# Units made by ScalarE, the second group's P5 and P4 by quarters, and a new written order, in a two-level Strassen matmul

## The chip, the cores and the metric

The kernel runs on one core of one Trainium2 chip. The metric is device time in microseconds of one execution, the median of three runs. A core has TensorE (PE in the profile: matmuls into PSUM; PEld: its weight loads), VectorE (DVE), ScalarE (ACT), GpSimd (POOL), and SyncE (SP), whose queue issues all DMAs of this kernel. A granted clock of 1.00 means TensorE at full speed.

## The reference

```python
x: (8, 2048, 2048) float32    w: (2048, 2048) float32
cs = cumsum(x, axis=1)
diff = cs - concatenate([zeros, cs[:, :-1, :]], axis=1)
out = matmul(diff, w)                       # float32
```

The difference of neighbouring running sums is x itself, so the output is x @ w: 16384 rows by 2048 by 2048.

## The kernel before

**Tiling.** The 16384 rows are 128 row tiles of 128 rows. The first four (the `plain` rows, L302) are multiplied in bf16 without further tricks while w arrives: the prologue, period 0. It makes an identity matrix on DVE (`zeros`, `ones`, `numbers`, `numbers turned`, four times `eye`, L220 to L236), loads x in pieces (`first x.q.r`, L245) and w in halves of 128x1024 (`w.h.ko`, L281), casts x (`cast x`, DVE, L251), turns it on PE against the identity (`turn x`, L260; `turned`, L270), casts w on ScalarE (L287), and takes the largest absolute value of w (`max w`, DVE, L291). From that maximum come `uw` and its reciprocal `uinv`. PE runs 30 `warm` matmuls of zeros (L338) in the gaps before. When uinv is there, w is scaled and written as fp16 in place: the blocks B11, B21, B12, B22 (`block`, L415 on DVE, L417 on ScalarE). `left over` (L430) is a last piece of the plain rows, made from blocks B11 and B21.

The other row tiles go in groups of four, g, g+1, h = g+2 and h+1. A group's rows times w is done by one level of the Strassen-Winograd scheme, seven products for two pairs of row tiles: A11 B11 (called P1), A12 B21 (P2), S1 T1 (P5), S4 B22 (P3), A22 T4 (P4), S2 T2 and S3 T3. S1 to S4 are sums of blocks of x, T1 to T4 of w. A product takes row tiles g and h with the same right operand. It is done in one of two ways. A `Whole` product is 32 matmuls of 128x512 (`matmuls`, L529). A `Quarters` product applies the same scheme once more, 28 matmuls (`quarter`, L551): seven slots of four matmuls, in exchange for DVE sums s1 to s4 of left operands, two DVE additions in PSUM (`middle`, `last`), three copies on ScalarE (`first`, `out2`, `out4`, L568), and differences of the right operand. Right operands that stay are made once (`make_1` to `make_5` of the class `Seven`); others are made anew for each group, into one buffer `flow`, by `give` (Q1, Q3, Q4). All these DVE operations are recorded through one helper at L517.

The first group (period 0) does all its products whole. In the second (period 1) P1, P5 and P4 are whole, P2 and P3 by quarters. From the third on, all five named are by quarters; S2 T2 and S3 T3 are whole throughout. Periods 1 to 30 are one group each, period 31 the tail.

**Around the products.** Each row tile is loaded in two halves (`load`, L130), weighed (`weigh`, ScalarE, L138: mean of absolute values, collected by an accumulator), given a `mean` (DVE, L157), a `scale` (DVE, L159) and a `unit` (L160): `unit` is the mean times `uw`, a 128x1 tile, and with it results are scaled back. ScalarE narrows the scaled tile to fp16 (`narrow`, L170), and a transposing DMA turns it (`turn`, L187). Results are taken from PSUM by ScalarE (`keep`, L565) and DVE (`add`, L576, multiply and add), and stored (`put`, L584 and L596). A name such as unit5 counts the row tile from the first of the group in work: 4 to 7 belong to the next group. `keep C11h.0` is the first half of C11 of row tile h, `C11h+P2.h.1` the addition of P2's second half to it, `P5.s3` a sum and `P5.4` a slot of P5.

**Order.** Every operation is recorded with a label, and `emit` sorts them by period times PERIOD plus a place from tables written out by hand: one each for the periods 0, 1, 2, 29, 30, 31, and one, `None`, for all the others. So each engine's instructions, and SP's DMAs, stand in the order of these tables. Semaphore waits follow from the operands.

```python
record(f"unit{role(t)}", "pool", lambda: nc.gpsimd.tensor_scalar(u, m, uw, None, MUL))
...
def all_seven(g):
    return g > PLAIN + 4
```

Of the kernel before, what the change touches and what calls it, by code (L numbers as in the profile page):

```python
# [10 lines left out]
def kernel(  # L11
# [6 lines left out]
    nc = tc.nc  # L18
# [26 lines left out]
    PERIOD = 1600  # L45
# [74 lines left out]
    def role(t):  # L120
        return t - PLAIN - 4 * period[0]
# [26 lines left out]
    def scale_of(t):  # L148
        if t < END:
            m2 = sums_of.pop(t)  # L150
            m = means_at[t % 4]
            s = scales[t] = scales_at[t % 8]
            u = unit[t] = units_at[t % 8]
            record(
                f"mean{role(t)}",
                "dve",
                lambda: nc.vector.tensor_scalar(m, m2[:, :1], m2[:, 1:], TINY, ADD, MAX),  # L157
            )
            record(f"scale{role(t)}", "dve", lambda: nc.vector.reciprocal(s, m))  # L159
            record(f"unit{role(t)}", "pool", lambda: nc.gpsimd.tensor_scalar(u, m, uw, None, MUL))  # L160
# [443 lines left out]
    class Seven:  # L604
# [13 lines left out]
        def room(self):  # L618
            return [spare.pop(0) for _ in range(4)]
# [244 lines left out]
    def all_seven(g):  # L864
        return g > PLAIN + 4
# [15 lines left out]
    def group(g):  # L881
# [62 lines left out]
        if more:  # L944
            P5 = Quarters("P5", P2.banks, S1g, S1h, in_5, room(at))
        else:
            P5 = Whole("P5", P2.banks, S1g, S1h, T1)
# [12 lines left out]
        if more:  # L960
            in_5.give("Q3")
# [58 lines left out]
        if more:  # L1020
            P4 = Quarters("P4", P3.banks, A22g, A22h, in_4, room(at))
            P4.one()
            P4.two()
        else:
            P4 = Whole("P4", P3.banks, A22g, A22h, T4)
        in_3.give("Q3")
        if not more:
            make_5(in_5)
# [19 lines left out]
        if more:  # L1048
            in_4.give("Q1")
# [19 lines left out]
        if more:  # L1069
            in_4.give("Q3")  # L1070
# [25 lines left out]
        if next_g < END:  # L1096
            if all_seven(g + 4) and more:
                in_1.give("Q1")
# [15 lines left out]
        if not more:  # L1114
            make_3(in_4)
            in_1.give("Q1")
# [11 lines left out]
    for g in range(PLAIN + 4, END, 4):  # L1128
# [8 lines left out]
            'first x.0.2': 0, 'first x.1.1': 1, 'first x.0.0': 2, 'first x.1.3': 3,  # L1137
            'first x.0.3': 4, 'first x.0.1': 5, 'first x.1.2': 6, 'first x.1.0': 7, 'w.0.0': 8,
            'zeros': 9, 'ones': 10, 'numbers': 11, 'numbers turned': 12, 'eye': 13, 'eye#2': 14,
# [390 lines left out]
```

## Time and profile before

| | |
|---|---|
| runs | 1452.06 us median (1451.21, 1452.06, 1452.2) |
| profiled execution, its own time | 1451.33 us |
| its span | 1449.5 us |
| PE | 1440.0 us busy, 6706 matmuls |
| DVE | 1339.7 us busy, 2457 instructions |
| ScalarE | 1129.8 us busy, 1742 instructions |
| GpSimd | 43.3 us busy, 129 instructions |
| granted clock | 1.000 |
| DMA | 351.60 MB, 243 GB/s mean |

The span is what the profiler saw, from the first to the last instruction or transfer; the execution's own time has some 1.8 us more around it. Busy times are a mean over stages with different limits, so what holds PE up is read from its waits and from windows of single stages. A line of the lines' view reads: code line, engine, operation, output and input tiles, shape, count, then busy time and mean ns of one, then the idle time before, and what ended it. In a timeline, the first two numbers are the start and the length, and a bracket at the end gives the idle time ahead and what released it.

### The profile page before, as it was taken

The numbers are of one execution on the slowest core, as the hardware profiler recorded it, in microseconds if no ns is written. First come the engines' busy times: TensorE is split into PE (matmuls) and PEld (weight loads), VectorE is DVE, ScalarE is ACT, GpSimd is POOL, SyncE is SP. The second block draws the span as 40 slices with busy tenths as digits, with TensorE's granted clock in tenths as the row PEclk, the third lists the DMA queues.
The fourth block names the chain that finished last, engine by engine and source line by source line (L and its number), as shares of the span: only waits on it lengthen the run. The fifth ranks groups of instructions, "written<-read, shape, count | busy, mean of one in ns | idle before, by whom it ended". The sixth has DMA issues, their size and how long they took to land.

```text
span 1449.5 us, 20480 instructions
## 1 busy us (share of the span) xinstructions
PE 1440.0 (99%) x6706; PEld 653.6 (45%) x6706; DVE 1339.7 (92%) x2457; ACT 1129.8 (78%) x1742; POOL 43.3 (3%) x129
## 2 busy tenths in 40 slices
PE   8999999999999999999999999999999999999998
PEld 4444444444444444444444444444444444444443
DVE  6998899999999999999999999999999999999998
ACT  5987678887778877778877788877788777788773
POOL 0000000000000000000000000000000000000000
PEclk9999999999999999999999999999999999999999
DMA  9999978999888899988898888998889988888973
GB/s 362 375 263 263 245 200 235 237 252 252 232 222 240 238 263 238 235 220 236 242 273 224 227 233 239 252 249 229 227 238 237 265 243 230 216 242 241 273 204 111
DMA packets 343788, 351.60 MB, mean 243 GB/s; under 512 B 270976, under 2 KB 270976, under 8 KB 343680
## 3 DMA queue, kind: packets, MB, share of 16 engines
q1 hardware_dynamic: 343680, 350.29, 88.5%
q8 instruction: 52, 0.85, 0.2%
q14 instruction: 56, 0.46, 0.1%
HBM read 150.99 MB, written 134.22 MB: 197 GB/s over the span
## 4 chain that ended last, share of the span: by engine, by line
PE 98%; DMA 2%; DVE 0%; ACT 0%; SPq 0%; issue 0%; DVEq 0%; ACTq 0%
PE b L551 61%; PE b L529 33%; PE b L302 3%; DMA W<-in_w_dram 1%; DMA W<-in_x_dram 0%; PE b L430 0%; DVE arena L576 0%; SPq L245 0%; ACT arena L287 0%; PE b L260 0%; DVE b L517 0%; ACT arena L565 0%; DVEq L1525 0%; ACTq L287 0%
## 5 line engine op out<-in xcount | busy, mean ns | idle before, releaser
L529 PE MATMUL b<-W,x 128*128 128x512 f16 x2176 | 532.5, 379 | 0.0
L576 DVE SCALAR_TENSOR_TENSOR arena<-b,tiny,arena 128x512 f32<-128x512 f32 x612 | 447.3, 745 | 12.8 <-PE b L529 2.9
L551 PE MATMUL b<-W,arena 128*128 128x512 f16 x1640 | 410.1, 379 | 0.0
L551 PEld LDWEIGHTS <-arena 128*128 128x128 f16 x2700 | 264.1, 98 | 318.6 <-DVE arena L517 0.2
L565 ACT ACTIVATE arena<-b,tiny 128x512 f32<-128x512 f32 x496 | 327.2, 687 | 54.6 <-PE b L529 29.5
L170 ACT ACTIVATE F<-F,tiny 128x1024 f16<-128x1024 f32 x246 | 282.6, 1149 | 61.9 <-DVE tiny L159 58.1
L529 PEld LDWEIGHTS <-x 128*128 128x128 f16 x2176 | 212.9, 98 | 256.7
L551 PE MATMUL b<-W,x 128*128 128x512 f16 x1180 | 289.0, 379 | 0.0
L138 ACT ACTIVATE waste<-F 128x1024 uint8<-128x1024 f32 x246 | 259.5, 1055 | 5.1 <-DMA F<-in_x_dram 3.2
L551 PE MATMUL b<-arena 128*128 128x512 f16 x1060 | 262.7, 379 | 0.0
L568 ACT COPY arena<-b 128x512 f32<-128x512 f32 x294 | 169.7, 577 | 89.4 <-PE b L551 66.4
L517 DVE TENSOR_TENSOR b<-b,arena 128x512 f32<-128x512 f32 x294 | 202.8, 691 | 31.6 <-ACT arena L565 29.6
L551 PEld LDWEIGHTS <-x 128*128 128x128 f16 x1416 | 138.6, 98 | 167.1
L517 DVE TENSOR_TENSOR arena<-W 128x2048 f16<-128x2048 f16 (+1 forms) x155 | 182.0, 1175 | 4.6 <-PE b L551 4.5
L568 ACT COPY b<-b 128x512 f32<-128x512 f32 x147 | 83.9, 571 | 85.1 <-PE b L551 61.6
L517 DVE TENSOR_TENSOR arena<-W,arena 128x512 f16<-128x512 f16 (+1 forms) x157 | 87.8, 563 | 6.7 <-PE b L551 6.6
L517 DVE TENSOR_TENSOR arena<-x,x 128x1024 f16<-128x1024 f16 (+1 forms) x180 | 89.1, 507 | 1.3 <-PE b L551 1.3
L517 DVE TENSOR_TENSOR x<-x,x 128x1024 f16<-128x1024 f16 x124 | 84.7, 684 | 1.0
L160 POOL TENSOR_SCALAR tiny<-tiny 128x1 f32<-128x1 f32 x124 | 42.7, 352 | 1303.2 <-DVE tiny L157 1295.3
L517 DVE TENSOR_TENSOR arena<-arena 128x512 f16<-128x512 f16 x116 | 49.2, 425 | 17.4 <-PE b L551 11.6
L551 PE MATMUL b<-arena,x 128*128 128x512 f16 x236 | 60.2, 379 | 0.0
L302 PE MATMUL b<-arena 128*128 128x512 bf16 x240 | 53.6, 379 | 2.3 <-ACT arena L287 1.4
(44 smaller groups left out, 513.9 us busy)
## 6 DMA issues: line engine op xcount, KB each, us to landing
F<-in_x_dram SPq DMA_DIRECT2D x246, 512.0 KB, 5.9
out_dram<-arena SPq DMA_DIRECT2D x240, 512.0 KB, 4.4
W<-in_w_dram SPq DMA_DIRECT2D x32, 512.0 KB, 9.6
out_dram<-arena SPq DMA_DIRECT2D x32, 256.0 KB, 3.2
W<-in_x_dram SPq DMA_DIRECT2D x16, 256.0 KB, 6.3
x<-F SPq DMA_TRANSPOSE x246, 4.6
arena<-in_x_dram SPq DMA_DIRECT2D x2, 512.0 KB, 5.3
x<-arena SPq DMA_TRANSPOSE x2, 5.4
```

The source lines that it names most:

```text
L138: lambda: nc.scalar.activation(waste, data, ABS, scale=1.0 / ROW, accum_out=m),
L160: record(f"unit{role(t)}", "pool", lambda: nc.gpsimd.tensor_scalar(u, m, uw, None, MUL))
L170: lambda: nc.scalar.activation(to, data, COPY, scale=s),
L302: said = nc.tensor.matmul(to[n], xP[:, r, ko, :], b[:, ds(n * NB, NB)], start=(ko == 0), stop=(ko == KO - 1),)
L517: record(label, "dve", lambda: nc.vector.tensor_tensor(dst, p, q, op))
L529: said = nc.tensor.matmul(to[n], a[k], b[k][:, n, :], start=(start and k == 0), stop=(k == KH - 1), skip_group_check=True,)
L551: said = nc.tensor.matmul(to, a[k], b[k], start=(start and k == 0), stop=(k == 3), skip_group_check=True)
L565: record(label, "act", lambda: nc.scalar.activation(c, p, COPY, scale=u))
L568: record(label, "act", lambda: nc.scalar.copy(to, p))
L576: label, "dve", lambda: nc.vector.scalar_tensor_tensor(c, p, u, c, MUL, ADD)
```

## The change

`unit` becomes an activation on ScalarE (a copy scaled by `uw`) in place of a GpSimd tensor_scalar; there are 124 of them. In the second group P5 and P4 become `Quarters` like P2 and P3, with what this asks for: make_5 and make_3 come earlier, the gives in_5.Q3, in_4.Q1 and in_4.Q3 are now made in that group too, in_1.Q1 moves ahead of the last slots, and P4's `last` falls into the following period. PERIOD grows, and all tables of places are new.

```diff
-    PERIOD = 1600
+    PERIOD = 1619
...
-            record(f"unit{role(t)}", "pool", lambda: nc.gpsimd.tensor_scalar(u, m, uw, None, MUL))
+            record(
+                f"unit{role(t)}",
+                "act",
+                lambda: nc.scalar.activation(u, m, COPY, scale=uw),
+            )
...
-        if more:
-            P5 = Quarters("P5", P2.banks, S1g, S1h, in_5, room(at))
-        else:
-            P5 = Whole("P5", P2.banks, S1g, S1h, T1)
+        P5 = Quarters("P5", P2.banks, S1g, S1h, in_5, room(at))
...
-        if more:
-            in_5.give("Q3")
+        if not more:
+            make_5(in_5)
+        in_5.give("Q3")
...
-        if more:
-            P4 = Quarters("P4", P3.banks, A22g, A22h, in_4, room(at))
-            P4.one()
-            P4.two()
-        else:
-            P4 = Whole("P4", P3.banks, A22g, A22h, T4)
+        P4 = Quarters("P4", P3.banks, A22g, A22h, in_4, room(at))
+        P4.one()
+        P4.two()
         in_3.give("Q3")
         if not more:
-            make_5(in_5)
+            make_3(in_4)
...
-        if more:
-            in_4.give("Q1")
+        in_4.give("Q1")
...
-        if more:
-            in_4.give("Q3")
+        in_4.give("Q3")
...
-            if all_seven(g + 4) and more:
+            if all_seven(g + 4):
                 in_1.give("Q1")
...
-        if not more:
-            make_3(in_4)
-            in_1.give("Q1")
```

Places that the prediction speaks of. At the start the old order is, on SP, eight pieces of x and then w; on DVE `numbers`, `eye`, then the casts. The new one, places in brackets, is on SP `w.0.2` (0), `first x.1.1` (1), `first x.0.1` (2), `first x.0.2` (3), `first x.1.0` (4), `first x.0.0` (5), and on DVE `zeros` (21), `ones` (22), `cast x.0.0` (23), `numbers` (45), `eye` (47). In the table for all other periods:

| operation | place before | place after |
|---|---|---|
| P2.5 (PE) | 1071 | 897 |
| C11g+P2.g.1, C11h+P2.h.0 | 1104, 1110 | 1020, 1019 |
| unit5, unit7 of the period before | 620, 1487 | 965, 995 |
| keep C11h.0, keep C11h.1 | 1093, 1192 | 997, 1012 |
| weigh4.0, weigh4.1 | 1094, 1134 | 1007, 1014 |
| mean4, scale4 | 1140, 1145 | 1022, 1031 |
| C11h+P2.h.1 | 1332 | 1028 |
| S1h | 1183 | 1108 |
| P5.s1, P5.s2 | 1184, 1185 | 1132, 1154 |
| S3h, S2h, S4h | 1350, 1488, 1489 | 1211, 1218, 1229 |
| P5.s4, P5.s3 | 1407, 1412 | 1243, 1264 |
| P5.4 (PE) | 1422 | 1296 |

More of the change, by code (lines that the diff above doesn't have):

```diff
@@ L1136 @@
         0: {
-            'first x.0.2': 0, 'first x.1.1': 1, 'first x.0.0': 2, 'first x.1.3': 3,
-            'first x.0.3': 4, 'first x.0.1': 5, 'first x.1.2': 6, 'first x.1.0': 7, 'w.0.0': 8,
-            'zeros': 9, 'ones': 10, 'numbers': 11, 'numbers turned': 12, 'eye': 13, 'eye#2': 14,
[64 rows of a table removed]
-            'max w.1.10': 330, 'max w.1.14': 333, 'max w.1.15': 335, 'max': 336, 'max of all': 338,
[74 rows of a table removed]
-        },
[45 rows of a table removed]
-        },
[43 rows of a table removed]
[4 rows of a table added]
+            'w.0.9': 20, 'zeros': 21, 'ones': 22, 'cast x.0.0': 23, 'cast w.0.2': 24,
[3 rows of a table added]
+            'warm.15': 42, 'warm.16': 43, 'numbers': 45, 'numbers turned': 46, 'eye': 47,
[49 rows of a table added]
+            'max w.1.15': 262, 'max w.1.14': 263, 'max': 264, 'max of all': 265, 'uw': 266,
[83 rows of a table added]
+        },
[48 rows of a table added]
+        },
[44 rows of a table added]
         },
         29: {
[42 rows of a table removed]
[41 rows of a table added]
         },
         30: {
[34 rows of a table removed]
[34 rows of a table added]
         },
         31: {
-            'P4.last': 455, 'C21h+P4.h.1': 456, 'put-1.0.1': 496, 'C21h+P4.h.0': 567,
-            'put-1.0.0': 1083,
+            'P4.last': 460, 'C21h+P4.h.1': 465, 'put-1.0.1': 471, 'C21h+P4.h.0': 635,
+            'put-1.0.0': 1021,
         },
         None: {
[42 rows of a table removed]
[43 rows of a table added]
         },
```

689 rows, old and new, of the table places are left out of this document.

## The prediction

> **What bounds the kernel now.** I read the page's head first, then the waits of PE, then the start, the windows of one stage each, one group of four row tiles in the steady stretch, and the end.
>
> ```profile
> span 1449.5 us, 20480 instructions
> PE 1440.0 (99%) x6706; PEld 653.6 (45%) x6706; DVE 1339.7 (92%) x2457; ACT 1129.8 (78%) x1742; POOL 43.3 (3%) x129
> ...
> L160 POOL TENSOR_SCALAR tiny<-tiny 128x1 f32<-128x1 f32 x124 | 42.7, 352 | 1303.2 <-DVE tiny L157 1295.3
> ```
>
> TensorE is busy for all but 9.5 us; DVE follows at 92%. The granted clock is 1.00 throughout. The units cost GpSimd 352 ns each, and its wait before them is for DVE: nobody is shown waiting for them. The waits of PE, with the total, the times and the longest:
>
> ```profile
> PE b L302 <- ACT arena L287: 1.4, 1, 1.4
> PE b L260 <- DVE W L251: 1.2, 1, 1.2
> PE b L338 <- DVE arena L229: 1.2, 1, 1.2
> PE b L302 <- DVE arena L270: 0.8, 1, 0.8
> ```
>
> All four lie in the first 27 us; after that PE never stops. So any matmul of the main part starts at the PE work in front of it plus one constant, the lag, here 12.52 us. A change moves the end in four ways only: PE's work, the lag at the start, a new stop later, and what follows the last matmul. The start, by time:
>
> ```profile
> 2.10 1.15 DVE L220 TENSOR_SCALAR waste<-W 32x128 bf16<-32x128 f32 x4
> 4.72 1.67 SPq L281 DMA_DIRECT2D W<-in_w_dram  x2
> 8.14 0.69 DVE L251 CAST W<-W 128x1024 bf16<-128x1024 f32 x1 [4.89 <-DMA W<-in_x_dram]
> 8.89 0.62 PE L260 MATMUL b<-waste,W 128*128 128x128 bf16 x8 [1.20 <-DVE W L251]
> ```
>
> DVE makes the identity (L220), has nothing for 4.89 us, casts the first piece of x, and PE turns it at 8.89; the first useful product begins at 12.97. Three stretches by window (PE, PEld, DVE, ACT, POOL busy, then clock and DMA):
>
> ```profile
> 60.00:100.00 40.00, 40.00 (x187) 18.09 (x185) 39.02 (x71) 36.38 (x52) 3.05 (x5) 1.00 1.06 275
> 100.00:165.00 65.00, 65.00 (x303) 29.48 (x302) 56.76 (x126) 44.42 (x67) 3.85 (x6) 1.00 0.94 243
> 254.00:298.00 44.00, 44.00 (x206) 19.92 (x205) 41.11 (x77) 35.00 (x56) 1.21 (x4) 1.00 0.93 237
> ```
>
> DVE is free for 1.0 us, 8.2 us and 2.9 us. One steady group, around the two slots that decide:
>
> ```profile
> 355.46 1.40 DVE L576 SCALAR_TENSOR_TENSOR arena<-b,tiny,arena 128x512 f32<-128x512 f32 x2
> 357.24 0.21 DVE L157 TENSOR_SCALAR tiny<-tiny 128x1 f32<-128x1 f32 x1 [0.37 <-ACT waste L138]
> 358.15 0.68 DVE L517 TENSOR_TENSOR arena<-x,x 128x1024 f16<-128x1024 f16 x1
> 358.87 0.88 DVE L517 TENSOR_TENSOR arena<-arena 128x512 f16<-128x512 f16 x2
> 362.02 0.42 DVE L517 TENSOR_TENSOR arena<-arena 128x512 f16<-128x512 f16 x1 [0.44 <-PE b L551]
> 362.69 1.03 PE L551 MATMUL b<-arena 128*128 128x512 f16 x4
> ```
>
> The last two are P5.s3 and P5.4: DVE's result is ready 0.25 us before PE takes it; a handover takes 0.06, so some 0.2 is spare. And the end:
>
> ```profile
> 1443.40 2.73 DVE L576 SCALAR_TENSOR_TENSOR arena<-b,tiny,arena 128x512 f32<-128x512 f32 x4
> 1443.58 1.03 PE L551 MATMUL b<-W,x 128*128 128x512 f16 x4
> ```
>
> PE ends at 1444.60, DVE at 1446.13, 1.53 later; the last output lands at 1448.71.
>
> **The change part by part.** The profiled execution took 1451.33 us, 0.73 under the median of 1452.06; the sum goes against 1451.33.
>
> *Work.* P5 and P4 of the group of period 1 lose 4 of 32 matmuls each. A matmul starts 0.2158 us after the one before, so 8 of them are **-1.73 us**, all on PE's path.
>
> *The start.* The new first table issues `w.0.2`, 512 KB, ahead of five pieces of x of 256 KB, and on DVE puts `cast x.0.0` ahead of `numbers` and `eye`, which stood before every cast. The first landings come evenly, 512 KB by 6.05 us and 256 KB more every 0.65 us; `first x.0.0` is now the sixth DMA, complete with 1792 KB landed, at about 9.3, where the first cast's pieces were there at 8.1. Cast 0.69, then the scan, transpose and four writes of the identity (0.42, 0.31, 1.15): eye at about 11.9, first turn 12.0 instead of 8.89. The other halves of x have landed by then, so the stretch to the first product shrinks: it starts at about 14.1 instead of 12.97. The 1.4 us stop for w's eighth half then closes, and the lag comes to 13.0. Later PE meets `left over.1`, which needs B11.7, and DVE makes the blocks B11 only after uinv is there, at 60.1. From the first block at 60.38, 14 blocks of 0.663 and two pairs of mean and scale (0.64) put B11.7 at 70.3 to 71.0. PE's work before `left over.1` is 244 matmuls of 0.2158 and 64 of 0.0755, 57.5 us: at a lag of 12.5 it would come at 70.0, at 13.0 at 70.5; it can go at 71.1. Lag 13.6, **+1.05**. If the blocks are not late, only the 0.5 of the lag stays; if DVE's order there has one more block ahead, +1.7.
>
> *Units to ScalarE.* 124 times 352 ns leave GpSimd, worth nothing: off the path, and no queue but GpSimd's own shortens. ScalarE gets four more instructions a group, 35.0 of 44.0 us being busy. Two, unit5 and unit7, now stand directly before keep C11h.0, weigh4.0, keep C11h.1, weigh4.1, on which mean4 on DVE waits. With steps from before (keep 0.58, weigh 1.045 and a mean no sooner than 1.18 after a weigh's start), weigh4.1 frees mean4 at 5.52 us after the start of P2.4 plus two units; DVE wants it at 6.04. A unit up to 0.26 us is therefore free. The trace has no such activation. Below: the 0.13 us that the accumulator's read adds between two weighs (1.17 against 1.04; its record is 191 ns). Above: GpSimd's 0.352 for the same 128x1. I take 0.2, by the row of ScalarE itself, so **0**. At 0.352 mean4 comes 0.18 late in each of 26 groups: +4.7.
> The Trainium skill, "ScalarE: Activation LUTs", section "What ACT_TABLE_LOAD costs", gives 186 ns plus 0.833 ns an element for an ACTIVATE, about 93 more for each pointer operand and 93 less back to back: an estimate of 0.19 here, by which the term is 0 too; no run shown here has a 128x1 activation.
>
> *P5 and P4 by quarters in period 1.* DVE gets 8 sums at 0.335, 4 PSUM adds at 0.60 and 3 differences of w at 1.135: 8.5 us; ScalarE 6 copies at about 0.47, 2.8 us of 20 free. make_5 and make_3 only move to an earlier place. Between 100 and 165 DVE has 8.2 us free and 1.5 more up to 210. Adding the steps in the new order from uinv on, the operands nearest to late are a difference of the next group's S1g (0.21 us spare), P5.4 (0.24) and P5.2 (0.43). I take **0**. If the stretch is short by the 0.3 that 8.5 exceeds 8.2, +0.3; if the sums wait in line behind gives, several such stops, up to +5.
>
> *The steady order.* S2h and S4h, which followed P5.4, now stand before P5.s4 and P5.s3, and C11h+P2.h.1 before S1h. The chain from P2.5 to P5.4: P2.5 ends and DVE starts after 1.06; then C11g+P2.g.1 0.66, mean4 0.12, C11h+P2.h.1 0.66, scale4 0.08, S1h 0.72, s1 0.46, s2 0.34, S3h 0.72, S2h 0.72, S4h 0.60, s4 0.33, s3 0.42, handover 0.06: 6.95 us. PE goes through eight pieces of 0.8633 meanwhile, 6.91. So 0.04 a group, in periods 3 to 28: **+1.1** (0 if the steps sum to 0.04 less; +3.6 at 0.1 more).
>
> *The end.* The new last tables put P4.4, two pieces of S3g T3.1 and P4.3, P4.5, P4.6 so that fewer of the last DVE additions queue up; by their steps the last ends 0.85 after PE instead of 1.53: **-0.7** (0 to -0.9; what follows it, 2.6 us of output, stays).
>
> The DMAs of the steady group are the same ones, in SP's queue at other places; no landing shows as a wait of PE there, and DMA load is 0.93: nothing.
>
> Sum: -1.73 + 1.05 + 0 + 0 + 1.1 - 0.7 = -0.3; 1451.0 for an execution like the profiled one, **1451.9** with most of the 0.73 to the median.
>
> **The rivals.**
>
> *No new wait.* The chain and the blocks fit after all. For it: 0.04 us is less than the spread of the steps, and uinv may land with the moved DMAs before 60.1. Against it: every step was read from this trace. Then -1.73 + 0.5 - 0.7: 1449.4 for the execution, 1450.1 for the median; still within 0.2%, since not more than -2.9 would be outside.
>
> *Units too dear (ends slower).* One mechanism: unit5 and unit7 ahead of weigh4 delay mean4. At 0.352 each, +4.7 on the forecast: 1456.6. It decides from 0.32 us a unit, where the 26 groups pay 0.12 each, 3.1 in all. For it stands GpSimd's row, against it the 191 ns of ScalarE's own shortest instruction.
>
> *DVE cannot hold period 1.* 8.5 us into 8.2 plus 1.5, with weighs and narrows also in that stretch: three or four stops of about a microsecond, 1455.5. Against it: the PE pieces there can be taken in other order, and the sum found 0.2 spare.
>
> *The clock falls.* PE now idles from about 9.3 to 12.0, 2.7 us; the longest gap of the trace is 1.57, and its clock stayed 1.00. In the beginning, the first 8 matmuls ran 0.427 us apart instead of 0.2158. If the gap causes this again, 8 matmuls are late by 1.7 in all, of which 0.5 goes into the wait for B11.7: 1453.1.
> The Trainium skill, "TensorE: Matmul & The Clock Gate", section "What's actually happening", says that the clock halves after an idle window of about 3.4 us; by that 2.7 us is not enough, and by it the sum is the forecast's.
>
> **How the numbers follow.** A measurement of this kernel cannot be told from no change within about 0.2%, 2.9 us: 1449.16 to 1454.96. Chances: forecast 0.60, no new wait 0.16 (a quarter of it below 1449.2), units too dear 0.09, DVE in period 1 0.08, clock 0.07. Faster: that quarter, 0.04, and 0.01 of the forecast, 0.05. Slower: units and period 1, 0.17; the clock's 1453.1 lies within. Same: 0.59 + 0.12 + 0.07 = 0.78. The range leaves out the lower part of the rival without waits and the dear units: 1449.4 to 1455.6. The likeliest case alone spans 1450.2 to 1453.9.
>
> **What would show it.** PE with 6698 matmuls, 124 more on ScalarE's activations and POOL nearly empty; an idle PE of 2.7 us before the first L260, ended by DVE; a wait of PE on DVE's blocks of about 0.5 near 71 us; some 26 waits of 0.04 at L551 for DVE L517; DVE ending 0.85 after PE; 8.5 us more DVE between 100 and 165. The prediction is wrong if a unit's step exceeds 0.26 us, if PE waits between 75 and 210, if the matmuls after 12 us run at 0.43, or if the waits per group are tenths.

## The result and the profile after

The changed kernel takes 1453.63 us (median of 22 runs, 1453.24 to 1454.73), the kernel before 1451.52 (22 runs): ratio 1.0014, 95% interval 1.0008 to 1.0021. That is 2.1 us slower, where a gain of 0.2 was forecast. The time lies inside the range and inside the 0.2% that were called no change, but the sign is wrong, and the interval is finer than that bound.

The head of the page, and from the groups kept apart by shape the unit on ScalarE:

```profile
span 1451.5 us, 20112 instructions
...
PE 1442.2 (99%) x6692; PEld 651.1 (45%) x6698; DVE 1349.6 (93%) x2472; ACT 1136.0 (78%) x1872; POOL 0.5 (0%) x5
```
```profile
L163 ACT ACTIVATE tiny<-tiny 128x1 f32<-128x1 f32 x124 | 33.2, 290 | 0.9 <-DVE tiny L157 0.9
```

The eight matmuls are gone (6698 weight loads; six matmul records are missing). A unit's record is 290 ns, but the next instruction of ScalarE starts 0.185 to 0.198 us after it in 116 of the 124 cases: the 0.2 that the sum used. The Trainium skill, "ScalarE: Activation LUTs", section "What ACT_TABLE_LOAD costs", had given an estimate of 0.19; the trace agrees.

The waits of PE:

```profile
PE b L264 <- DVE waste L224: 1.7, 1, 1.7
PE b L342 <- DVE arena L233: 1.2, 1, 1.2
PE b L306 <- DVE arena L274: 0.8, 1, 0.8
PE b L306 <- issue: 0.2, 1, 0.2
```

This view lists only the long ones. The small waits were taken from the distance between the starts of neighbouring matmuls: whatever is over 0.2158 us. Most stops cost a little more than the stop itself, since the matmul behind it, too, starts 0.01 us late. After 165 us all this sums to 2.55 us in the changed kernel and to 0 in the one before. The start, by time, and the windows around it (PE, PEld, DVE, ACT, POOL busy, clock, DMA):

```profile
9.78 0.69 DVE L255 CAST W<-W 128x1024 bf16<-128x1024 f32 x1 [8.52 <-DMA W<-in_x_dram]
...
11.18 1.16 DVE L224 TENSOR_SCALAR waste<-W 32x128 bf16<-32x128 f32 x4
12.37 1.29 DVE L255 CAST W<-W 128x1024 bf16<-128x1024 f32 x2
12.40 1.35 PE L264 MATMUL b<-waste,W 128*128 128x128 bf16 x16 [1.74 <-DVE waste L224]
```
```profile
12.00:13.00 1.00, 0.60 (x8) 0.43 (x7) 0.95 (x4) 0.45 (x1) 0.00 (x0) 1.00 1.00 408
13.00:14.00 1.00, 0.62 (x9) 0.45 (x8) 0.89 (x3) 0.81 (x2) 0.00 (x0) 0.89 1.03 416
14.00:15.00 1.00, 0.47 (x2) 0.20 (x3) 1.00 (x2) 0.83 (x1) 0.00 (x0) 0.50 1.07 399
15.00:16.00 1.00, 1.00 (x8) 0.72 (x7) 0.34 (x2) 0.00 (x0) 0.00 (x0) 0.50 1.00 403
16.00:17.00 1.00, 0.84 (x5) 0.51 (x5) 1.00 (x2) 0.55 (x1) 0.00 (x0) 0.50 1.02 404
17.00:18.00 1.00, 0.93 (x5) 0.44 (x5) 0.55 (x1) 1.00 (x2) 0.00 (x0) 0.90 1.05 410
```

The identity is ready at 12.34 us and the first turn starts at 12.40, some 0.4 later than forecast. What had been the rival of the smallest chance happened too: the clock falls to 0.50 for 3.4 us, from 13.78 to 17.19. The first product starts at 14.53. The first product of the first group, with the same matmuls ahead of it, starts 1.15 us later than before; here it is before and after:

```profile
71.74 2.75 PE L529 MATMUL b<-W,x 128*128 128x512 f16 x12
```
```profile
72.89 1.89 PE L533 MATMUL b<-W,x 128*128 128x512 f16 x8
```

So the lag is 13.67 here, where it was 12.52.

From uinv (60 us) to 165 us, before and after, in one window each:

```profile
60.00:165.00 105.00, 105.00 (x489) 47.57 (x487) 95.78 (x196) 80.81 (x119) 6.91 (x11) 1.00 0.99 255
```
```profile
60.00:165.00 105.00, 104.95 (x487) 47.23 (x487) 103.90 (x215) 84.94 (x134) 0.05 (x1) 1.00 0.97 251
```

DVE went from 95.78 to 103.90 of 105 us: it has 1.1 us free left. A steady group, around the same two slots as before:

```profile
358.13 0.20 DVE L157 TENSOR_SCALAR tiny<-tiny 128x1 f32<-128x1 f32 x1
...
358.25 0.74 DVE L580 SCALAR_TENSOR_TENSOR arena<-b,tiny,arena 128x512 f32<-128x512 f32 x1
...
361.93 0.69 DVE L521 TENSOR_TENSOR x<-x,x 128x1024 f16<-128x1024 f16 x1
...
362.54 0.75 DVE L521 TENSOR_TENSOR arena<-arena 128x512 f16<-128x512 f16 x2
...
363.35 0.82 PE L555 MATMUL b<-arena 128*128 128x512 f16 x3
```

P5.s4 and P5.s3 (362.54) end at 363.29, P5.4 starts at 363.35: PE waits for them, 0.05 us in each of 26 groups, 0.06 with the late start of the matmul behind. And the end:

```profile
1444.17 3.39 DVE L580 SCALAR_TENSOR_TENSOR arena<-b,tiny,arena 128x512 f32<-128x512 f32 x5 [0.33 <-PE b L533]
...
1445.70 1.03 PE L555 MATMUL b<-W,x 128*128 128x512 f16 x4
```

PE ends at 1446.73, DVE at 1447.56, 0.83 later as forecast. But the span goes on for 3.90 us from there, where it was 3.42.

Set against the profiled execution of before, with the lag as the prediction used it (a matmul's start less the PE work in front of it):

| term, us | forecast | measured |
|---|---|---|
| work | -1.73 | -1.73 |
| lag at 76 us, 12.52 before | +1.05 | +1.15 (13.67) |
| waits from 76 to 165 us | 0 | +0.15 |
| waits at P5.4 in 26 groups | +1.1 | +1.55 |
| waits at 1405 to 1418 us | 0 | +0.72 |
| other waits, at 669, 672, 1233 and 1245 us | 0 | +0.28 |
| DVE's end after PE's | -0.7 | -0.70 |
| span's end after DVE's | 0 | +0.48 |
| sum | -0.3 | +1.9 (execution +1.91) |

### The profile page after: what moved, and what is told of

It reads as the page before. It is cut to its first block, busy times and chain, and to the rows that moved or that the text cites. A ratio compares the mean times of both kernels' runs of the same rounds, so it can differ in the third digit from the quotient of the medians.

```text
span 1451.5 us, 20112 instructions
## 1 busy us (share of the span) xinstructions
PE 1442.2 (99%) x6692; PEld 651.1 (45%) x6698; DVE 1349.6 (93%) x2472; ACT 1136.0 (78%) x1872; POOL 0.5 (0%) x5
## 4 chain that ended last, share of the span: by engine, by line
PE 97%; DVE 1%; DMA 1%; issue 0%; ACT 0%; SPq 0%; DVEq 0%; ACTq 0%
PE b L555 61%; PE b L533 32%; PE b L306 4%; DMA F<-in_x_dram 1%; DMA W<-in_x_dram 0%; DVE arena L580 0%; PE b L264 0%; PE b L434 0%; DVE arena L521 0%; ACT F L174 0%; SPq L249 0%; DVE W L255 0%; DVE b L521 0%; DVE waste L224 0%; DVE arena L274 0%
## 5 line engine op out<-in xcount | busy, mean ns | idle before, releaser
L533 PE MATMUL b<-W,x 128*128 128x512 f16 x2144 | 513.2, 379 | 0.0
L580 DVE SCALAR_TENSOR_TENSOR arena<-b,tiny,arena 128x512 f32<-128x512 f32 x612 | 442.0, 744 | 11.0 <-PE b L555 5.1
L555 PE MATMUL b<-W,arena 128*128 128x512 f16 x1672 | 414.4, 379 | 0.2
L555 PE MATMUL b<-W,x 128*128 128x512 f16 x1192 | 295.9, 379 | 0.0
L555 PE MATMUL b<-arena 128*128 128x512 f16 x1072 | 270.3, 379 | 0.1
L572 ACT COPY arena<-b 128x512 f32<-128x512 f32 x298 | 173.2, 581 | 107.0 <-PE b L555 63.4
L521 DVE TENSOR_TENSOR arena<-W 128x2048 f16<-128x2048 f16 (+1 forms) x158 | 186.1, 1179 | 23.9 <-PE b L555 23.0
L521 DVE TENSOR_TENSOR arena<-x,x 128x512 f16<-128x512 f16 (+1 forms) x181 | 89.9, 509 | 1.1 <-PE b L555 0.7
L521 DVE TENSOR_TENSOR arena<-arena,x 128x512 f16<-128x512 f16 x119 | 49.9, 421 | 1.8
L521 DVE TENSOR_TENSOR arena<-x,arena 128x512 f16<-128x512 f16 x119 | 49.9, 420 | 0.6 <-PE b L555 0.6
```

The costliest lines, as they stand in the source:

```text
L521: record(label, "dve", lambda: nc.vector.tensor_tensor(dst, p, q, op))
L533: said = nc.tensor.matmul(to[n], a[k], b[k][:, n, :], start=(start and k == 0), stop=(k == KH - 1), skip_group_check=True,)
L555: said = nc.tensor.matmul(to, a[k], b[k], start=(start and k == 0), stop=(k == 3), skip_group_check=True)
L572: record(label, "act", lambda: nc.scalar.copy(to, p))
L580: label, "dve", lambda: nc.vector.scalar_tensor_tensor(c, p, u, c, MUL, ADD)
```

## The experiments

Each edit is made in the changed kernel unless something else is said. To set the profiles side by side: gap is the time between the starts of the last `warm` matmul and the first turn; lag at 165 us is 12.52, plus what the last matmul starts later than in the kernel before, plus 1.73 for the eight matmuls, less all waits after 165 us; lag at 76 us is that less the waits from 76 to 165 us.

| kernel | gap | clock at 0.5 | lag at 76 | lag at 165 |
|---|---|---|---|---|
| before | 1.57 | none | 12.52 | 12.52 |
| changed | 2.12 | 3.4 us | 13.67 | 13.82 |
| eye_first | 1.46 | none | 13.26 | 13.69 |
| b11_early | 2.14 | 6.8 us | 15.22 | 15.22 |
| eye_and_b11 | 1.24 | none | 13.20 | 13.74 |
| s4h_later | 2.29 | 6.8 us | 15.58 | 15.58 |
| s4h_after_middle | 3.14 | 6.8 us | 14.77 | 14.77 |
| units_pool | 3.05 | 6.8 us | 14.58 | 14.58 |
| reordered | 1.01 | none | 12.38 | 13.43 |
| fewer_adds | 1.13 | none | 12.07 | 12.09 |
| four_mended | 0.92 | none | 13.27 | 14.00 |

Each row is one execution. The kernels eye_and_b11, reordered, fewer_adds and four_mended, all explained below, have the same order up to 72 us, and their lags at 76 us still lie 1.2 us apart: a difference of some tenths at 76 us says nothing.

### The start: eye_first, b11_early and both

After the first look at the traces my theory was that two causes stood side by side: the late, half-clocked start, and B11.7, which ended at 71.20 us. The matmul that reads it started at 71.81, so PE could come only 0.55 us sooner without waiting for it. The expectations of these three runs take 14.0 for the lag of the changed kernel; it is 13.67.

```diff
-'cast x.0.0': 23
+'cast x.0.0': 50.5          # behind the fourth eye, 50
```

> The changed kernel with one place altered: `cast x.0.0` behind the fourth `eye` on DVE. Theory (two causes side by side): the identity is ready by 4 us, the gap of PE ahead of the first turn closes, and the granted clock stays at 1.00 after 13 us; but B11.7 still ends at about 71.2 us, so the lag of PE falls only from 14.0 to 13.9 us and a wait of PE at `left over.1` appears: 1453.5 us. Rival (the start alone sets the lag): the lag falls to about 12.5, 1452.1 us.

1452.81 us, ratio to before 1.0008 (0.9999 to 1.0016), between the theory and the rival. The clock stays at 1.00. The lag is 12.97 at 72 us; at 74.4 us PE waits 0.30 for a block of B21 on DVE, which makes the lag 13.26, and at S1g T1 (87.4 us) 0.22 for S1g on DVE.

```diff
-'B11.6': 570, 'B11.4': 587, 'B11.7': 596, 'mean2': 583, 'scale2': 584
+'B11.6': 499.2, 'B11.4': 499.4, 'B11.7': 499.6, 'mean2': 521, 'scale2': 521.5
-'B21.4': 503, 'B21.6': 659, 'B21.5': 662
+'B21.4': 522, 'B21.6': 649, 'B21.5': 649.5
```

> The changed kernel with B11.6, B11.4 and B11.7 ahead of the B21 blocks on DVE (and B21.5, B21.6 ahead of B12.7). Theory (two causes side by side): B11.7 ends at about 67 us, but PE came out of the start 14.0 us late anyway: lag 14.0, 1453.6 us, no gain. Rival (the blocks set the lag): it falls to about 12.5, 1452.1 us.

1454.23 us, ratio 1.0017 (1.0008 to 1.0026): no gain. Its profile holds a longer stretch at half clock (lag 15.2), so it says nothing finer.

> Both edits of the start. Theory (two causes side by side): only now the lag falls, to between 12.4 and 12.9 us, 1452.1 to 1452.5 us. Rival (either one alone sets the lag): the same time as with that one alone.

1452.48 us, ratio 1.0007 (0.9998 to 1.0015). The time is near what the theory gave, but not for its reason: the lag at 76 us is 13.20, hardly lower than with the first edit alone, and the wait at S1g T1 is now 0.33. S1g ends at 87.37 and PE starts at 87.43, where the kernel before started that product at 86.42. So a third operand brings the lag to 13.5. Two single causes did not explain it. The new theory: DVE has hardly a gap from 60 to 165 us (103.99 of 105 us busy), so no operand's place matters much; whatever is moved ahead, another comes late.

### DVE from 60 to 165 us: reordered, fewer_adds and t4_on_pool

`reordered` has both edits above and

```diff
-'S1g': 1075, 'mean3': 1076, 'scale3': 1077, 'S1h': 1130
+'S1g': 1065.5, 'mean3': 1078.5, 'scale3': 1078.6, 'S1h': 1115.5
-'T3.2': 1064, 'T2[4:].2': 1058, 'T3.6': 1116
+'T3.2': 1089.6, 'T2[4:].2': 1088.5, 'T3.6': 1130.5
```

> Both edits of the start, and on DVE S1g ahead of C11g+V.0, S3g ahead of mean3, S1h ahead of mean4, with T3.2, T2[4:].2 and T3.6 put off. Theory (DVE has work without a gap from uinv at 60 us to 165 us, and that, no single operand, holds the lag at 13.5): the wait at S1g T1 at 87.4 us goes, but waits of 0.3 to 0.9 us in all come up between 95 and 145 us; the lag after 165 us stays at 13.5 to 13.7, and the time at 1452.5. Rival (S1g alone is late): lag 12.6 to 12.9 to the end, 1451.7.

1452.82 us, ratio 1.0007 (0.9998 to 1.0016). The wait at 87.4 us is gone and the lag at 76 us is 12.38; then PE waits 0.52 at 93.7, 0.30 at 113.0, 0.05 at 118.2, 0.11 at 129.6 and 0.06 at 139.1 us, 1.04 in all. The lag at 165 us is 13.43. Near the theory's numbers (waits of 0.3 to 0.9, lag 13.5 to 13.7), not the rival's.

```diff
 # in reordered, in group_plain
-        add("C11g+V", C11g, V, ug)
-        add("C11h+Z", C11h, Z, uh)
-        add("C12g+V", C12g, V, ug)
-        add("C22+X", C22, X, vg)
-        add("C22+Y", C22, Y, vh)
-        add("C12h+Z", C12h, Z, uh)
```

> The reordered kernel without the 12 additions of PSUM parts into C of the first group (C11g+V to C22+Y; the results of that group lack those parts), 12 of 0.66 us off DVE between 82 and 135 us. Theory (DVE saturated from 60 to 165 us): the waits at 93.7, 113, 129.6 and 139 us go, the lag after 165 us is 12.6 to 12.9 where it was 13.7, 1451.6 to 1451.9. Rival (single operands late by their place): the waits stay, 1452.8.

The 12 additions are left out, so the results of the first group lack those parts. 1451.82 us, ratio 1.0000 (0.9991 to 1.0009). Its window:

```profile
60.00:165.00 105.00, 105.00 (x489) 47.55 (x487) 97.96 (x203) 85.67 (x135) 0.00 (x0) 1.00 0.99 255
```

With 7 us free on DVE again, all those waits go but one of 0.02, and the lag at 165 us is 12.09. Of the 1.04, the 0.30 at 113.0 was a wait for one of the additions that are now missing, so it went with it; the other four, 0.74, were for operands that are still made. They show that DVE's load, not one late operand, holds the lag up by 165 us. The rest of the distance to `reordered`, 0.31, was there at 76 us already.

`t4_on_pool` is `reordered` with

```diff
-        less("T4", T4, B21, T2)
+        for k in range(KH):
+            def late(k=k):
+                return nc.gpsimd.tensor_tensor(T4[k], B21[k], T2[k], SUB)
+
+            record(f"T4.{k}", "pool", late)
```

> As the kernel with that order, with the eight differences T4 on GpSimd, 8 of 0.60 us off DVE. Theory (DVE saturated from 60 to 165 us): now the lag after 165 us falls to 12.6 to 13.0, 1451.7 to 1452.0. Rival (S1g alone is late): the same as without this edit. If GpSimd's transfers through the same memory slow DVE, its operations between 90 and 115 us are longer than 0.60 us a step, and the gain is less.

1465.95 us, ratio 1.0096 (1.0082 to 1.0110), far past what I had allowed for. Its timeline:

```profile
89.10 4.97 POOL L828 TENSOR_TENSOR W<-W 128x1024 f16<-128x1024 f16 x2 [28.50 <-DVE W L521]
89.47 2.62 DVE L521 TENSOR_TENSOR x<-arena,x 128x1024 f16<-128x1024 f16 x1
...
92.12 2.50 DVE L521 TENSOR_TENSOR x<-x,x 128x1024 f16<-128x1024 f16 x1
...
98.32 9.45 POOL L828 TENSOR_TENSOR W<-W 128x1024 f16<-128x1024 f16 x4 [4.24 <-DVE W L521]
...
101.23 4.56 DVE L521 TENSOR_TENSOR W<-W 128x512 f16<-128x512 f16 x2
...
105.71 2.61 DVE L521 TENSOR_TENSOR x<-x,x 128x1024 f16<-128x1024 f16 x1
```

A difference takes GpSimd about 2.5 us, and a DVE operation of 0.68 us beside it lasts 2.5 to 2.6: DVE is held until GpSimd is done. The Trainium skill, "GPSIMD Engine Reference", section "1. Specifications", says that the two share their SBUF interfaces and contend where DVE has two SBUF inputs; the trace agrees.

### The steady groups: s4h_later, s4h_after_middle

```diff
-'S4h': 1229
+'S4h': 1264.5               # s4h_later: behind P5.s3, 1264
+'S4h': 1288.5               # s4h_after_middle: behind P5.middle, 1288
```

> The changed kernel with S4h behind P5.s3 on DVE in the table of the other periods. Theory (DVE's chain from P2.5 to P5.4 is 0.05 us longer than PE's work beside it): 0.60 us leave the chain, the 26 waits at P5.4 go, and the longer ones of two groups with them: 1.3 to 1.6 us less, 1452.0 to 1452.3. Rival (the stop moves to the next operand, P3.s1, which needs S4h): waits of the same kind at P3.1, 1453.6 us.

1456.50 us, ratio 1.0032 (1.0020 to 1.0043). The wait at P5.4 is gone, but one of 0.165 us stands at P5.5 in each group; neither theory had named it:

```profile
364.70 0.42 DVE L521 TENSOR_TENSOR arena<-arena 128x512 f16<-128x512 f16 x1 [0.41 <-PE b L555]
365.05 0.68 DVE L521 TENSOR_TENSOR x<-x,x 128x1024 f16<-128x1024 f16 x1
...
365.65 0.69 DVE L521 TENSOR_TENSOR b<-b,arena 128x512 f32<-128x512 f32 x1
...
366.39 0.81 PE L555 MATMUL b<-W,arena 128*128 128x512 f16 x3
```

P5.s3 (364.70) overwrites the buffer of s1, which P5.1 reads until 364.67, so it cannot be earlier than that. S4h (365.05) behind it pushes P5.middle (365.65), and P5.5 needs that. So S4h must go one step further.

> The changed kernel with S4h behind P5.middle on DVE in the table of the other periods, so that neither P5.s3 nor P5.middle stands behind it. Theory (DVE's chain from P2.5 to P5.4 is 0.05 us longer than PE's work beside it): no wait left at P5.4 or P5.5 in the steady groups, 1.3 to 1.6 us less than the changed kernel, 1452.0 to 1452.4. Rival (DVE's order in a group has no room at all, so the wait comes back at P3.1): 0.05 or more a group again, 1453.6 or above.

1452.13 us, ratio 1.0001 (0.9992 to 1.0010), by the medians 1.5 under the changed kernel. In its trace two waits are left after 76 us, 0.12 and 0.04: the 26 waits, 1.55 us by the trace of the changed kernel, are gone. The time is the theory's, but the medians do not show the 26 waits alone: in this profile the waits after 1400 us, 0.72 in the changed kernel's, are missing as well, and the lag at 165 us is 0.95 higher, with a longer half clock.

### The units: units_pool, units_on_act_in_before

```diff
 # units_pool
-            record(f"unit{role(t)}", "act", lambda: nc.scalar.activation(u, m, COPY, scale=uw))
+            record(f"unit{role(t)}", "pool", lambda: nc.gpsimd.tensor_scalar(u, m, uw, None, MUL))
 # units_on_act_in_before: the same the other way round, in the kernel before
```

> The changed kernel with the 124 units back on GpSimd, all else as changed. Theory (a unit takes ScalarE 0.19 us a step and stands beside other work): the 26 waits stay at 0.05 us, 1453.6. Rival (units on ScalarE hold mean4 up): the waits go, 1452.3 or below.

1453.97 us, ratio 1.0015 (1.0007 to 1.0024): the 26 waits stay at 0.05. Units on ScalarE cost nothing in the new order, and taking them from GpSimd gains nothing that these runs show.

> The kernel before with only the 124 units on ScalarE, its own tables kept. Theory (a unit steps 0.19 us on ScalarE, beside other work): no wait of PE after 35 us, 1451.5 us. Rival (units before a keep or weigh hold the adds up): waits at L551 in each group, of 0.1 us or more, 1454 or above.

1452.64 us, ratio 1.0006 (0.9997 to 1.0015), by the medians 0.9 over the kernel before. The steady groups have no wait, as expected. But against the expectation PE waits 0.72 at 193.24 us, once, in P3.1 of period 2, for ScalarE: unit6 waits there for mean6 until 188.43, with P5.out4, two narrows and the keeps behind it, and keep C12g.1 ends at 193.19 only, which PE has waited for. Two more waits, 0.04 and 0.18, stand at 681 and 683 us. So a unit is free only where ScalarE's queue has room, and in that one place of the old table it had none.

### The end: two_puts_less

```diff
 def put_half(c, t, h, n):
+    if (role(t), h, n) in ((1, 1, 0), (3, 1, 0)):
+        return
```

> The changed kernel without the stores put1.1.0 and put3.1.0 of the last group (256 KB of the output each is not written). Theory (the last stores come 0.66 us apart, 256 KB each, faster than they are written, and queue): the last store lands 2.5 us after its issue instead of 3.05, and the span ends 3.4 us after DVE instead of 3.9. Rival (the longer landing has another cause): 3.05 and 3.9 stay.

Two stores are left out. The rival: the last store still lands after 3.07 us (one execution), the span ends 4.05 us after DVE. Those two stores do not cause the longer landing. In every profile of the new order the first of the last five lands after 2.4 to 2.5 us and the next four after 2.8 to 3.2; in the two profiles of the old order the last four take 2.3 to 2.6 at the same distance of 0.66. What makes the difference stays open.

### The mends together: four_mended

Both edits of the start, S4h behind P5.middle, and in the table of period 29

```diff
-'mean7': 2854, 'scale7': 2855
+'mean7': 2976.3, 'scale7': 2976.4     # behind the first in1.Q4 of the next group
```

The last is for the waits at 1405 to 1418 us. Their chain, in order of time, in the changed kernel:

```profile
1396.36 7.35 DMA F<-in_x_dram
...
1404.76 0.20 ACT waste L138
1404.96 0.02 issue
1404.98 0.22 DVE tiny L157
...
1405.39 0.33 DVE arena L521
```

load7.1 is issued at 1396.36 and lands 7.35 us later; weigh7.1 waits for it, and mean7 (L157) for that, with P2.s2 and all the rest of DVE behind it. Before, load7.1 went out at 1395.16 and took 4.8, and mean7 stood behind P2.s2. The other half, load7.0, now goes out 1.25 us ahead of it; before, it was 3.5 us. In the profiles of the new order it takes 6.0 to 7.5; in the three with 6.0 to 6.2 the waits are not there.

> The changed kernel with four mends: `cast x.0.0` behind `eye`, B11.7 early, S4h behind P5.middle, and in the table of period 29 mean7 and scale7 behind the first in1.Q4 of the last group on DVE. Theory (the parts add up): clock 1.00 from 10 us on, lag 13.5 set by DVE's work after uinv, no waits at P5.4, no stop between 1400 and 1420 us however late load7.1 lands: last matmul at 1443.6, 1450.6 to 1451.0 us, 0.5 to 0.9 under the kernel before. Rival (a mend opens other waits, as S4h did): 1451.5 or more.

1450.69 us (11 runs, 1450.18 to 1452.12) against 1451.72, ratio 0.9995 (0.9986 to 1.0003). By the medians it beats both kernels, by 1.0 and 2.9 us; the interval against the kernel before still holds 1. Its trace has the clock at 1.00, no wait at P5.4, and load7.1 with 7.34 us to land leaves one wait of 0.21 at 1404.0 where there were three, 0.70 together. The lag at 165 us is 14.0, after waits of 0.73 for DVE from 76 us on: most of the 1.73 of the eight matmuls is still lost there. No run has the new order with P5 and P4 whole in period 1, so what these quarters alone cost or win is not measured.

## Why the prediction was wrong

*Work and end of DVE: right.* -1.73 and -0.70, as worked out.

*The steady order: right in its place, mis-sized.* The chain from P2.5 to P5.4 was to be 6.95 against 6.91, a stop of 0.04. PE waits 0.049 in each of 26 groups and the matmul behind starts 0.01 late: 1.55 for the forecast 1.1. s4h_after_middle confirms the place. At 672 and 1245 us the wait was longer, 0.12 and 0.09, and others stood ahead of it at 669 and 1233 us, 0.12 and 0.05: 0.28 more in all. They were not foreseen, and their cause stays open.

*Units: right.* 0.19 a step, no cost in this order.

*"No landing shows as a wait of PE there ... nothing": wrong at one place, and the largest miss.* The stretch read for it was the steady one. In period 29 the new table issues load7.1 close behind load7.0, it lands 2.6 us slower, and mean7, which waits for it, now stands in front of P2.s2 on DVE: 0.72.

*"What follows it, 2.6 us of output, stays": wrong by 0.48.* The stores that follow take 3.05 us to land, by a cause that stays open.

*The lag, +1.05: the number right by luck.* It was added up from a start that gives 13.0 and a wait of about 0.5 near 71 us for B11.7. No such wait is in the trace. B11.7 ended at 71.20, near the 71.0 of the forecast, but the sum lets `left over.1` begin with it, and the matmul that reads it is the fourth of that piece, at 71.81. The lag of 13.67 came whole out of the start, 3.4 us of it at half clock; in the five profiles with the identity first and the clock kept it was 12.1 to 13.3 at 72 us.

*P5 and P4 by quarters, "I take 0": wrong in its mechanism, by little in this execution.* The step set 8.5 us of new DVE work against 8.2 free between 100 and 165 and 1.5 after it, and looked for the operand nearest to late. But the two kernels need DVE in the same 105 us after uinv, and 103.9 of them are now used: work cannot be moved in front of uinv, nor behind the products that need it. In the changed kernel PE comes so late out of the start that only 0.15 of waits follow. Where it comes earlier, waits for DVE take the gain back: the lag at 165 us ends at 13.4 to 14.0 with each mended start (eye_first, eye_and_b11, reordered, four_mended), and at 12.1 once 7.9 us are taken off DVE. The eight matmuls win 1.73; a lag of 0.9 to 1.5 over the kernel before gives most of it back.

*The clock, chance 0.07: it happened, and in most runs.* All six profiles with the cast ahead of the identity show a gap of 2.1 to 3.1 us and then a half clock. In this one it lasted 3.4 us, and the lag at 165 us is only some 0.1 over that of eye_first (13.82 against 13.69). In the other five it lasted 6.8 us, and the lag stayed at 14.6 to 15.6. In the 22 runs of the changed kernel the mean granted clock is 0.999 in six, all at 1453.48 us or less, and 0.997 or 0.998 in the others, up to 1454.73. eye_first's median is lower, 1452.81; how much of that difference is the clock's and how much load7.1's, the medians do not say. The page of the Trainium skill that the prediction set against this rival, "TensorE: Matmul & The Clock Gate", section "What's actually happening", asks for an idle window of some 3.4 us; here gaps of 2.1 were enough.

The misses are 0.10 and 0.15 up to 165 us, 0.45 and 0.28 in the steady groups, 0.72 and 0.48 at the end: 2.2 us, the distance from -0.3 to +1.9. No large term was wrong; four terms set to nothing were not nothing, and all misses fell to the same side. The time before that the 0.73 was added for came out 0.5 lower over 22 runs, which brought the forecast in microseconds nearer than its sign.

## What to carry to other kernels

When matmuls are traded for work on another engine, sum that engine's work from the moment its first operand exists to the last product that needs it, and compare it with the PE time of the same stretch: a stretch with no gap left holds PE back, and moving single operations only moves the wait. An order that is full must be read for every queue that stands behind a moved instruction: S4h behind P5.s3 made the kernel 3 us slower, one operation further 1.5 faster. And a term set to zero because a steady stretch hides it is to be checked at the first and last group, where other tables and later loads hold.

## What the runs showed of the hardware

- A gap of 2.1 to 3.1 us between matmuls at the start was followed by a clock of 0.50 in all six profiles that had one, for 3.4 us in one and 6.8 in five; gaps of 0.9 to 1.6, in seven others, were not. t4_on_pool, with gaps of 1.9 and 2.0 in a row, lost its clock too.
- In every profile the changes of the granted clock lie whole multiples of 3.413 us apart, so it is not the gap alone that decides but how much of one such stretch it empties. In the stretch ahead of each of the eight falls during the work (those six, and two in t4_on_pool), matmuls were busy for at most 45% (in the changed kernel 1.51 of 3.41 us, from 10.37 to 13.78); no stretch with 49% or more was followed by a fall (eye_first, 1.66 of 3.41 us from 11.40 to 14.81). What brings the clock back after one stretch or after two is not shown: with 71% busy in the first one, the changed kernel took one and b11_early two.
- While GpSimd runs a 128x1024 difference of 2.5 us, a DVE operation with two inputs from the same memory lasts 2.5 us instead of 0.68. Units of 128x1 on GpSimd (352 ns) had no such effect: DVE's operations beside them are no longer than others.
- A load of 512 KB issued 1.25 us behind another one took 6.0 to 7.5 us to land, from profile to profile; issued 3.5 us behind it, 4.8 and 5.0 in the two profiles of the old order. The DMAs behind it differ too, so the cause is not shown.
